# Opening of a decoder trunk's first FFN: order of scaling, high part, low part and modulation

## The chip, the cores and the metric

The kernel runs on one core of one Trainium2 chip. The metric is device time in microseconds (us) of one execution, from the profiler's clock. The time given for a kernel is the median of several executions; one further execution is profiled and gives the trace. Engine names: PE is TensorE (matmuls and transposes), ACT is ScalarE, DVE is VectorE, POOL is GpSimd, SP is the engine that issues the DMAs.

## The reference, cut to what matters

Two decoder layers on one sequence of 512 rows with 1024 channels; each layer is FFN, token mixer, FFN. Every sub-layer normalizes its input and modulates it by shift and scale that come from a conditioning vector. Only the start of the first FFN matters here:

```
cond = silu(c)
mod  = (cond @ ada_w[i] + ada_b[i]).reshape(b_, N_SUBLAYERS, 3, D_MODEL)
h = rms_norm(x, norm_g[i, 0]) * (1.0 + mod[:, 0, 1]) + mod[:, 0, 0]
g, u = jnp.split(h @ ffn_w_in[i, 0], 2, axis=-1)
x = x + 0.5 * (1.0 + mod[:, 0, 2]) * ((silu(g) * u) @ ffn_w_out[i, 0])
```

All is float32. The kernel keeps the precision by splitting each operand in a high part (rounded to the matmul's format) and a low part (what is left), and by three matmuls per product: high by high, low by high, high by low.

## The kernel before, in words

Channels lie on the 128 partitions, in KT = 8 groups kt of 128; the 512 rows lie along the free dimension, in four blocks b of 128. `hhi[:, kt]` and `hlo[:, kt]` are the high and low part of the modulated input of group kt. The FFN's hidden channels come in units j of 128, each with a gate half and an up half (k = 0, 1), so each unit needs two PSUM banks of 128x512 for its sums over kt.

There are eight PSUM banks. `bank("s")` takes one of three (pool `pss`), `bank("mm")` one of five (pool `ps`). A bank is free for the next tile when the last instruction that uses the one before it is done.

The opening (L724 to L793) runs as follows.

- L724 to L731: SP issues the loads of the rows (four blocks of 128x1024), of the identity, of the conditioning vector, of the first modulation weights and of the small vectors.
- L733 to L738: ACT squares the rows and sums them, DVE and POOL make the scale `v` of each row.
- L762 to L767: the row blocks are scaled by `v`, all 1024 channels at once, blocks 1 and 3 on ACT, 0 and 2 on DVE.
- `ada_work` (L97 to L103) and `ada_affine` (L113 to L122), both on DVE, make the modulation of one channel group from 1 MB of weights: two products with sums of 128x1024 and three tiny instructions. The last, L122, writes the shift `ms`.
- `by_channel(kt)` (L756): PE transposes the four 128x128 blocks of group kt into an `s` bank, and ACT copies the bank to SBUF (`x[:, kt]`, L760).
- `some_weights(kt, first, last)` (L744): for the units j from first to last, SP loads the weights of the groups kt and kt + 1 (256 KB), ACT makes their high part (L752), DVE their low part (L753).
- The loop over kt (L772 to L787): ACT makes `t1` from the copy with scale and shift (L774) and rounds it to `hhi` (L776); at kt = 0 the weights of units 2 and 3 and the copy of group 1 follow; then the transposes and copy of group kt + 2, the modulation of group kt + 1, and after it, on DVE, `hlo` (L785); at even kt then the weights of the next two groups, all four units.
- L788 to L793: eight banks for the sums of units 0 to 3, and 192 matmuls: for each kt 4 units x 2 halves x 3 matmuls (`mm3`, L163 to L165). The first three banks (unit 0 both halves, unit 1 the gate half) are `s` banks, the other five `mm` banks. The `s` pool hands out its banks in the order of the requests, so the three sums come after the eight transposed groups.

What sets the order: SP, DVE and ACT run their instructions in the order in which the program writes them (L718, `manual_schedule`); each engine waits at the first instruction that is not ready. PE's order is made when the kernel is built, by a planner that works with estimated times; on the chip PE runs that list in order.

After the opening, `ffn` (L258) goes on: the first four units are gated (`gated`, L286), then each further unit takes its weights from `Feed`, which loads them (L157) and splits them (L151 on ACT, L152 on DVE) into the slots that earlier units free, and `up` makes 48 matmuls per unit.

Of the kernel before, what the change touches and what calls it, by code (L numbers as in the profile page):

```python
# [7 lines left out]
F32 = mybir.dt.float32  # L8
F32R = mybir.dt.float32r
AF = mybir.ActivationFunctionType  # L10
ALU = mybir.AluOpType
# [4 lines left out]
P = 128  # L16
D = 1024
KT = D // P
S = 512
# [21 lines left out]
def trunk(  # L41
# [6 lines left out]
    pe, act, dve, gp = nc.tensor, nc.scalar, nc.vector, nc.gpsimd  # L48

    top = ctx.enter_context(tc.tile_pool(name="top", bufs=1, side="right"))  # L50
    hhi = top.tile([P, KT, S], F32R, name="hhi")
    hlo = top.tile([P, KT, S], F32R, name="hlo")
# [12 lines left out]
    def bank(tag="mm"):  # L65
        return banks[tag].tile([P, S], F32, tag=tag, name=tag)
# [11 lines left out]
    ident = pers.tile([P, P], F32, name="ident")  # L78
    ng = pers.tile([P, DEPTH * 3, KT], F32, name="ng")
    ab = pers.tile([P, DEPTH * 3, 3 * KT], F32, name="ab")  # L80
    x = pers.tile([P, KT, S], F32, name="x")
# [8 lines left out]
    mods = {}  # L90

    def ada_load(i, u, pool):
        raw = pool.tile([P, 2, D], F32, tag="ada", name="ada")
        nc.sync.dma_start(raw, ada_w[i, u])
        return raw
# [620 lines left out]
    with tc.tile_pool(name="more", bufs=1, side="right", reuse_waits="tile") as more:  # L716
        slots.update(pools=[wts, wts, more], at=1)
        in_order = tc.manual_schedule(  # L718
            engines={mybir.EngineType.SP, mybir.EngineType.DVE, mybir.EngineType.Activation})
        with tc.tile_pool(name="start", bufs=2, reuse_waits="tile") as sp, in_order, ExitStack() as early:  # L720
            adas0 = early.enter_context(tc.tile_pool(name="adas", bufs=5, reuse_waits="tile"))
            w4 = early.enter_context(tc.tile_pool(name="w4", bufs=1, reuse_waits="tile"))

            rows = sp.tile([P, NTB, D], F32, name="rows", bufs=1)  # L724
            for b in range(NTB):
                nc.sync.dma_start(rows[:, b], x_rows[:, b])
            nc.sync.dma_start(ident, consts[:, 0])
            nc.sync.dma_start(cond, c_in.to_broadcast([P, D]))
            first_ada = ada_load(0, 0, adas0)
            nc.sync.dma_start(ng, norm_g)  # L730
            nc.sync.dma_start(ab, ada_b)  # L731
            v = sp.tile([P, NTB], F32, name="v", bufs=1)
            for b in range(NTB):  # L733
                junk = x[:, 2 * b:2 * b + 2].rearrange("p a t -> p (a t)")
                act.activation(junk, rows[:, b], AF.Square, accum_out=v[:, b:b + 1])
            act.activation(cond, cond, AF.Silu)
            dve.tensor_scalar(out=v, in0=v, scalar1=1.0 / D, scalar2=EPS, op0=ALU.mult, op1=ALU.add)
            gp.tensor_tensor(out=v, in0=v, in1=mhalf[:, :NTB], op=ALU.pow)  # L738
            wt = [slot([P, 2, KT, P]) for _ in range(3)]
            wt.append(tuple(w4.tile([P, 2, KT, P], F32R, name="w" + t) for t in "hl"))  # L740

            pieces = {}

            def some_weights(kt, first=0, last=4):  # L744

                sl = slice(kt, kt + 2)
                if first == 0:
                    pieces[kt] = wts.tile([P, 4, 2, 2, P], F32, tag="raw", name="raw")
                for j in range(first, last):
                    (wh, wl), raw = wt[j], pieces[kt][:, j]  # L750
                    nc.sync.dma_start(raw, w_in[0, j, :, :, sl])
                    act.activation(wh[:, :, sl], raw, AF.Copy)  # L752
                    dve.tensor_tensor(out=wl[:, :, sl], in0=raw, in1=wh[:, :, sl].bitcast(F32),  # L753
                                      op=ALU.subtract)

            def by_channel(kt):  # L756
                t = bank("s")
                for b in range(NTB):
                    pe.transpose(t[:, b * P:(b + 1) * P], rows[:, b, kt * P:(kt + 1) * P], ident)
                act.activation(x[:, kt], t, AF.Copy)  # L760

            for b in range(NTB):  # L762
                if b % 2:
                    act.activation(rows[:, b], rows[:, b], AF.Copy, scale=v[:, b:b + 1])
                else:
                    dve.tensor_scalar(out=rows[:, b], in0=rows[:, b], scalar1=v[:, b:b + 1],
                                      scalar2=None, op0=ALU.mult)  # L767
            ada_work(0, 0, first_ada)
            ada_affine(0, 0, 1)
            by_channel(0)  # L770
            some_weights(0, 0, 2)
            for kt in range(KT):  # L772
                t1 = sp.tile([P, S], F32, tag="t1", name="t1")
                act.activation(t1, x[:, kt], AF.Identity, scale=mods[0]["a"][:, kt:kt + 1],  # L774
                               bias=mods[0]["s"][:, kt:kt + 1])
                act.activation(hhi[:, kt], t1, AF.Copy)  # L776
                if kt == 0:
                    some_weights(0, 2)
                    by_channel(1)
                if kt + 2 < KT:  # L780
                    by_channel(kt + 2)
                if kt + 1 < KT:
                    ada_work(0, kt + 1, ada_load(0, kt + 1, adas0))
                    ada_affine(0, kt + 1, 1)
                dve.tensor_tensor(out=hlo[:, kt], in0=t1, in1=hhi[:, kt].bitcast(F32), op=ALU.subtract)  # L785
                if kt % 2 == 0 and kt + 2 < KT:
                    some_weights(kt + 2)  # L787
            gu = [[bank("s" if 2 * j + k < 3 else "mm") for k in range(2)] for j in range(4)]  # L788
            for kt in range(KT):
                for j in range(4):  # L790
                    for k in range(2):
                        mm3(gu[j][k], wt[j][0][:, k, kt], wt[j][1][:, k, kt], hhi[:, kt], hlo[:, kt],
                            kt == 0, kt == KT - 1)  # L793

        def begin(g, gated):
            for j in range(4):
                gated(gu[j], g[j], 0, S)

        ahead = []

        def normed(i, w):
            def then(acc, t0, tn):
                if t0 and w is not None:
                    ahead.append(Feed(w))
                    ahead[0].fetch(len(slots["pools"]))
                norm(i, acc, t0, tn)

            return then

        with tc.tile_pool(name="poolw", bufs=1, side="right", reuse_waits="tile") as pw:  # L810
            pw_all = pw.tile([P, 16, P], F32, name="poolw")
            pooling = []
            opened = ExitStack()

            def pool_then(acc, t0, tn):
                r = rsig(acc, t0, tn)
                if t0 == 0:
                    pool = opened.enter_context(tc.tile_pool(name="pool", bufs=1, reuse_waits="tile"))
                    pooling.append(Pooling(1, pool, pw_all))
                    pooling.append(pooling[0].means(r, t0, tn))  # L820
                    return
                sums = pooling[0].mix(pooling[1], *HALVES[0])
                made = pooling[0].means(r, t0, tn)
                norm(2, sums, *HALVES[0], True)
                sums = pooling[0].mix(made, t0, tn)
                ahead.append(Feed(1))
                ahead[0].fetch(len(slots["pools"]))
                norm(2, sums, t0, tn, True)
                opened.close()

            jobs = ada_jobs(0, False) + ada_jobs(1)
            jobs += [(lambda pool: nc.sync.dma_start(pw_all, pool_w), lambda _: None)] + ada_jobs(2)
            feed = Feed(0)
            feed.units = feed.units[4:]
            ffn(0, feed, jobs, pool_then, begin, started=4)
        ffn(2, ahead.pop(), ada_jobs(3) + ada_jobs(4), normed(3, 2))
        fox_early = ctx.enter_context(tc.tile_pool(name="foxe", bufs=2, reuse_waits="tile"))
        first, first_jobs = fox_first(fox_early)
        held = []

        def fox_then(acc, t0, tn):
            if t0:
                held.append(lambda: norm(4, acc, t0, tn))
            else:
                norm(4, acc, t0, tn)

        ffn(3, ahead.pop(), ada_jobs(5) + first_jobs, fox_then, ahead_by=1)
# [68 lines left out]
```

## Time and profile before

| | |
|---|---|
| median of 3 executions | 1816.23 us (1815.08 to 1818.02) |
| profiled execution, its own time | 1816.93 us |
| its span, first to last instruction | 1815.2 us |
| PE busy | 1780.4 us, 98% of the span |
| DVE busy | 990.0 us, 55% |
| ACT busy | 622.1 us, 34% |

The profile lists for each instruction the start, the duration, the line, what it writes and reads, and how long its engine stood idle before it and which engine or DMA ended that. The span leaves out what lies before the first and after the last instruction, so it is 1.7 us below the execution's time. Shares of busy time are means over the whole span; a change in one stretch is read from the instructions of that stretch.

### The profile page before, as it was taken

Reading aid. Unit: us, or ns where it says so; the run is one execution under the profiler, and the core shown is the slowest. Engines: PE = TensorE matmul, PEld = TensorE weight load, DVE = VectorE, ACT = ScalarE, POOL = GpSimd, SP = SyncE. Lnnn points to the kernel's source line nnn. Section 1 sums busy time; section 2 is a strip of 40 time slices with the busy share of each in tenths; the row PEclk is TensorE's granted clock in tenths of the full one; section 3 lists DMA queues with packets and bytes.
Section 4 is the critical chain, followed back from the end, with each engine's and each line's share of the span. In section 5 each row is a group of like instructions: output and inputs, shape, how many; then the busy total and the mean of one; then the engine's idle time right before and its main releaser. Section 6 shows DMA issues by size and latency. Waiting matters only on the chain.

```text
span 1815.2 us, 24017 instructions
## 1 busy us (share of the span) xinstructions
PE 1780.4 (98%) x9564; PEld 1533.2 (84%) x9564; DVE 990.0 (55%) x1963; ACT 622.1 (34%) x1258; POOL 107.3 (6%) x118
## 2 busy tenths in 40 slices
PE   6999999989999999999999999999999999999999
PEld 4888888889888888998888889989998888888887
DVE  7567566376466563373544543667777653433333
ACT  6323223344223222242232232355554442222231
POOL 0000000050000000110000001311110200000000
PEclk9999999989999999999999999999999999999999
DMA  9457466220457453123353442112222121331421
GB/s 366 194 197 279 174 231 245 94 70 30 152 215 276 163 210 138 71 86 124 140 208 116 177 160 81 52 55 72 80 71 76 47 93 60 130 110 49 139 93 70
DMA packets 45857, 244.73 MB, mean 135 GB/s; under 512 B 5409, under 2 KB 10017, under 8 KB 21937
## 3 DMA queue, kind: packets, MB, share of 16 engines
q1 hardware_dynamic: 45744, 243.20, 36.6%
q8 instruction: 75, 1.23, 0.3%
q14 instruction: 38, 0.30, 0.1%
HBM read 241.05 MB, written 2.13 MB: 134 GB/s over the span
## 4 chain that ended last, share of the span: by engine, by line
PE 94%; DVE 4%; ACT 1%; DMA 1%; issue 0%; POOL 0%; SPq 0%; DVEq 0%; ACTq 0%; POOLq 0%
PE mm L164 27%; PE mm L165 27%; PE mm L163 27%; PE s L163 3%; PE s L164 3%; PE s L165 2%; PE mm L593 1%; DVE wl L152 1%; PE mm L619 1%; PE mm L596 1%; PE mm L422 1%; DVE x L225 0%; DMA rows<-x_rows 0%; DVE t L387 0%; DVE win L396 0%
## 5 line engine op out<-in xcount | busy, mean ns | idle before, releaser
L164 PE MATMUL mm<-hlo,wh 128*128 128x512 f32 (+1 forms) x1512 | 560.7, 372 | 2.8 <-DVE hlo L785 2.8
L165 PE MATMUL mm<-hhi,wl 128*128 128x512 f32 (+1 forms) x1512 | 558.3, 372 | 0.5 <-DVE wl L152 0.5
L163 PE MATMUL mm<-hhi,wh 128*128 128x512 f32 (+1 forms) x1512 | 554.4, 372 | 2.1 <-ACT hhi L776 1.8
L151 ACT ACTIVATE wh<-raw 128x256 fp32r<-128x256 f32 (+2 forms) x528 | 311.5, 654 | 567.4 <-PE mm L164 308.6
L152 DVE TENSOR_TENSOR wl<-raw,wh 128x256 fp32r<-128x256 f32 (+2 forms) x528 | 359.6, 735 | 52.3 <-ACT wh L151 48.1
L164 PEld LDWEIGHTS mm<-hlo,wh 128*128 128x128 f32 x1512 | 284.6, 188 | 52.3 <-DVE hlo L785 3.4
L163 PEld LDWEIGHTS mm<-hhi,wh 128*128 128x128 f32 x1512 | 282.8, 189 | 52.5 <-ACT hhi L776 2.0
L165 PEld LDWEIGHTS mm<-hhi,wl 128*128 128x128 f32 x1512 | 284.5, 188 | 49.9 <-DVE wl L152 0.7
L290 DVE TENSOR_TENSOR sil<-sil,mm 128x512 f32<-128x512 f32 (+1 forms) x95 | 61.0, 642 | 463.1 <-PE mm L165 454.5
L164 PE MATMUL mm<-gl,wh 128*128 128x512 f32 (+1 forms) x848 | 299.1, 353 | 0.0
L165 PE MATMUL mm<-gh,wl 128*128 128x512 f32 (+1 forms) x848 | 298.4, 353 | 0.0
L163 PE MATMUL mm<-gh,wh 128*128 128x512 f32 (+1 forms) x848 | 297.9, 354 | 0.0
L164 PEld LDWEIGHTS mm<-gl,wh 128*128 128x128 f32 x848 | 160.4, 189 | 21.9
L165 PEld LDWEIGHTS mm<-gh,wl 128*128 128x128 f32 x848 | 160.4, 189 | 21.8
L163 PEld LDWEIGHTS mm<-gh,wh 128*128 128x128 f32 x848 | 159.7, 189 | 22.0
L100 DVE CUSTOM_DVE_ANT_0 ada<-ada,cond 128x1024 f32<-128x1024 f32 x144 | 170.2, 1220 | 0.5 <-DMA ada<-ada_w 0.5
L289 ACT ACTIVATE sil<-mm 128x512 f32<-128x512 f32 (+1 forms) x94 | 52.7, 560 | 245.1 <-PE mm L165 243.9
L337 DVE SCALAR_TENSOR_TENSOR x<-mm,mg,x 128x512 f32<-128x512 f32 x64 | 48.0, 750 | 103.2 <-PE mm L165 102.2
L175 POOL TENSOR_TENSOR acc<-acc,sq 128x256 f32<-128x256 f32 x56 | 49.8, 889 | 845.0 <-ACT sq L174 513.9
L163 PE MATMUL s<-wh,hhi 128*128 128x256 f32 x288 | 84.6, 294 | 0.0
L165 PE MATMUL s<-wh,hlo 128*128 128x256 f32 x288 | 82.0, 285 | 0.0
L164 PE MATMUL s<-wl,hhi 128*128 128x256 f32 x288 | 81.9, 285 | 0.0
(173 smaller groups left out, 1633.7 us busy)
## 6 DMA issues: line engine op xcount, KB each, us to landing
raw<-w_in SPq DMA_DIRECT2D x84, 1024.0 KB, 4.9
ada<-ada_w SPq DMA_DIRECT2D x72, 1024.0 KB, 4.9
raw<-w_out SPq DMA_DIRECT2D x64, 512.0 KB, 5.6
raw<-w_end SPq DMA_DIRECT2D x12, 1024.0 KB, 4.9
raw<-fox_qkv SPq DMA_DIRECT2D x12, 1024.0 KB, 4.8
raw<-w_in SPq DMA_DIRECT2D x16, 256.0 KB, 8.0
cb<-cum SPq DMA_DIRECT2D x16, 256.0 KB, 3.4
raw<-fox_o SPq DMA_DIRECT2D x4, 1024.0 KB, 4.9
```

The source lines that it names most:

```text
L100: dve.tensor_tensor_reduce(out=raw[:, r, :], in0=raw[:, r, :], in1=cond, scale=1.0, scalar=0.0, op0=ALU.mult, op1=ALU.add, accum_out=mods[ ...
L151: act.activation(hi[:, c:c + n], src[:, c:c + n], AF.Copy)
L152: dve.tensor_tensor(out=lo[:, c:c + n], in0=src[:, c:c + n], in1=hi[:, c:c + n].bitcast(F32), op=ALU.subtract)
L163: pe.matmul(o, lh, rh, start=start, stop=False)
L164: pe.matmul(o, lh, rl, start=False, stop=False)
L165: pe.matmul(o, ll, rh, start=False, stop=stop)
L175: gp.tensor_tensor(out=acc[:, sl], in0=acc[:, sl], in1=sq, op=ALU.add)
L289: act.activation(sil[:, :tn], gu[0][:, :tn], AF.Silu)
L290: dve.tensor_tensor(out=sil[:, :tn], in0=sil[:, :tn], in1=gu[1][:, :tn], op=ALU.mult)
L337: done = dve.scalar_tensor_tensor(out=x[:, dt, :], in0=y, scalar=mods[i]["g"][:, dt:dt + 1], in1=x[:, dt, :], op0=ALU.mult, op1=ALU.add)
L422: pe.matmul(y[:, :tn], self.w[:, 2 * dt + ct], made[dt // 2][:, ct], start=ct == 0, stop=ct == 1)
L593: pe.matmul(s[hh][:, :n], self.q[m == 2][rows, self.pair, b * P:n], self.k[m == 1][rows, self.pair, :n], start=m == 0, stop=False)
```

## The change

Seven edits, all in the opening. Rows are scaled in two steps: first the channels 0 to 255 of all four blocks, then, later and all on ACT, the other 768 (blocks 1 and 3 ahead of the first modulation, blocks 0 and 2 at the end of kt = 0). The copy of each transposed bank to SBUF goes. `hhi` is made by one ACT instruction straight from the PSUM bank (`high`), and `t1` by a second one from the same bank (`whole`). The first `high` stands between the weights of unit 0 and unit 1. `hlo` moves ahead of the next group's modulation. The weights of the later groups are split two units at a time: units 0 and 1 of groups kt + 1 and kt + 2 at odd kt, units 2 and 3 at the even kt that follows, in both cases ahead of `hlo`.

```diff
-            def some_weights(kt, first=0, last=4):
+            def some_weights(kt, first, last, between=None):
...
                     act.activation(wh[:, :, sl], raw, AF.Copy)
                     dve.tensor_tensor(out=wl[:, :, sl], in0=raw, in1=wh[:, :, sl].bitcast(F32),
                                       op=ALU.subtract)
+                    if between and j == first:
+                        between()
 
             def by_channel(kt):
-                t = bank("s")
+                turned[kt] = bank("s")
                 for b in range(NTB):
-                    pe.transpose(t[:, b * P:(b + 1) * P], rows[:, b, kt * P:(kt + 1) * P], ident)
-                act.activation(x[:, kt], t, AF.Copy)
-
+                    pe.transpose(turned[kt][:, b * P:(b + 1) * P], rows[:, b, kt * P:(kt + 1) * P], ident)
+
+            def scaled(b, c0, c1, on_act):
+                part = rows[:, b, c0:c1]
+                if on_act:
+                    act.activation(part, part, AF.Copy, scale=v[:, b:b + 1])
+                else:
+                    dve.tensor_scalar(out=part, in0=part, scalar1=v[:, b:b + 1], scalar2=None, op0=ALU.mult)
+
+            def high(kt):
+                act.activation(hhi[:, kt], turned[kt], AF.Identity, scale=mods[0]["a"][:, kt:kt + 1],
+                               bias=mods[0]["s"][:, kt:kt + 1])
+
+            def whole(kt):
+                t1 = sp.tile([P, S], F32, tag="t1", name="t1")
+                act.activation(t1, turned.pop(kt), AF.Identity, scale=mods[0]["a"][:, kt:kt + 1],
+                               bias=mods[0]["s"][:, kt:kt + 1])
+                return t1
+
+            turned = {}
+            soon = 2 * P
             for b in range(NTB):
-                if b % 2:
-                    act.activation(rows[:, b], rows[:, b], AF.Copy, scale=v[:, b:b + 1])
-                else:
-                    dve.tensor_scalar(out=rows[:, b], in0=rows[:, b], scalar1=v[:, b:b + 1],
-                                      scalar2=None, op0=ALU.mult)
+                scaled(b, 0, soon, b % 2)
+            by_channel(0)
+            for b in (1, 3):
+                scaled(b, soon, D, True)
             ada_work(0, 0, first_ada)
             ada_affine(0, 0, 1)
-            by_channel(0)
-            some_weights(0, 0, 2)
+            some_weights(0, 0, 2, lambda: high(0))
+            by_channel(1)
             for kt in range(KT):
-                t1 = sp.tile([P, S], F32, tag="t1", name="t1")
-                act.activation(t1, x[:, kt], AF.Identity, scale=mods[0]["a"][:, kt:kt + 1],
-                               bias=mods[0]["s"][:, kt:kt + 1])
-                act.activation(hhi[:, kt], t1, AF.Copy)
+                if kt:
+                    high(kt)
+                t1 = whole(kt)
+                if kt % 2 and kt + 1 < KT:
+                    some_weights(kt + 1, 0, 2)
+                elif kt % 2 == 0 and kt:
+                    some_weights(kt, 2, 4)
+                dve.tensor_tensor(out=hlo[:, kt], in0=t1, in1=hhi[:, kt].bitcast(F32), op=ALU.subtract)
                 if kt == 0:
-                    some_weights(0, 2)
-                    by_channel(1)
+                    some_weights(0, 2, 4)
+                    for b in (0, 2):
+                        scaled(b, soon, D, True)
                 if kt + 2 < KT:
                     by_channel(kt + 2)
                 if kt + 1 < KT:
                     ada_work(0, kt + 1, ada_load(0, kt + 1, adas0))
                     ada_affine(0, kt + 1, 1)
-                dve.tensor_tensor(out=hlo[:, kt], in0=t1, in1=hhi[:, kt].bitcast(F32), op=ALU.subtract)
-                if kt % 2 == 0 and kt + 2 < KT:
-                    some_weights(kt + 2)
```

## Rows read from the trace of the kernel before

**Rows 1.** The page's first line: span.

```profile
span 1815.2 us, 24017 instructions
```

**Rows 2.** Stretches from:to: length, PE, PEld, DVE, ACT, POOL busy, clock, DMA share, GB/s.

```profile
0.00:28.64 28.64, 11.62 (x49) 8.67 (x49) 16.02 (x36) 19.20 (x30) 1.31 (x6) 0.94 0.98 356
28.64:68.66 40.02, 40.02 (x177) 32.62 (x177) 25.54 (x54) 18.58 (x31) 0.00 (x0) 1.00 0.47 183
```

**Rows 3.** Timeline of PE: start, duration, instruction, [idle before, what ended it].

```profile
17.70 2.26 PE L163 MATMUL mm<-hhi,wh 128*128 128x512 f32 x5 [1.78 <-ACT hhi L776]
19.76 1.91 PE L759 MATMUL s<-ident,rows 128*128 128x128 f32 x8
22.89 0.50 PE L164 MATMUL mm<-hlo,wh 128*128 128x512 f32 x1 [1.22 <-DVE hlo L785]
...
28.64 0.50 PE L164 MATMUL mm<-hlo,wh 128*128 128x512 f32 x1 [1.57 <-DVE hlo L785]
...
36.13 0.39 PE L163 MATMUL s<-hhi,wh 128*128 128x512 f32 x1
...
68.66 0.48 PE L163 MATMUL mm<-hhi,wh 128*128 128x512 f32 x1
```

**Rows 4.** Timeline of DVE in the opening, same columns.

```profile
13.24 1.23 DVE L100 CUSTOM_DVE_ANT_0 ada<-ada,cond 128x1024 f32<-128x1024 f32 x1 [0.46 <-DMA ada<-ada_w]
...
15.93 0.15 DVE L122 COPY ms<-mraw 128x1 f32<-128x1 f32 x1
...
19.41 1.22 DVE L100 CUSTOM_DVE_ANT_0 ada<-ada,cond 128x1024 f32<-128x1024 f32 x1
...
22.15 0.68 DVE L785 TENSOR_TENSOR hlo<-t,hhi 128x512 fp32r<-128x512 f32 x1
22.75 2.49 DVE L753 TENSOR_TENSOR wl<-raw,wh 128x512 fp32r<-128x512 f32 x4
25.16 1.22 DVE L100 CUSTOM_DVE_ANT_0 ada<-ada,cond 128x1024 f32<-128x1024 f32 x1
...
27.84 0.15 DVE L122 COPY ms<-mraw 128x1 f32<-128x1 f32 x1
27.90 0.68 DVE L785 TENSOR_TENSOR hlo<-t,hhi 128x512 fp32r<-128x512 f32 x1
28.50 1.22 DVE L100 CUSTOM_DVE_ANT_0 ada<-ada,cond 128x1024 f32<-128x1024 f32 x1
```

**Rows 5.** Timeline of ACT in the opening, same columns.

```profile
15.10 1.14 ACT L752 ACTIVATE wh<-raw 128x512 fp32r<-128x512 f32 x2
...
28.02 0.81 ACT L774 ACTIVATE t<-x,ms,ma 128x512 f32<-128x512 f32 x1 [3.66 <-DVE ms L122]
28.87 0.63 ACT L776 ACTIVATE hhi<-t 128x512 fp32r<-128x512 f32 x1
29.41 0.58 ACT L760 ACTIVATE x<-s 128x512 f32<-128x512 f32 x1
...
37.11 0.82 ACT L774 ACTIVATE t<-x,ms,ma 128x512 f32<-128x512 f32 x1 [3.18 <-DVE ms L122]
```

**Rows 6.** Groups by line and form, ACT: count | busy us, mean ns | idle before.

```profile
L752 ACT ACTIVATE wh<-raw 128x512 fp32r<-128x512 f32 x16 | 9.2, 623 | 0.3
L774 ACT ACTIVATE t<-x,ms,ma 128x512 f32<-128x512 f32 x8 | 6.5, 812 | 11.9 <-DVE ms L122 11.9
L776 ACT ACTIVATE hhi<-t 128x512 fp32r<-128x512 f32 x8 | 5.1, 632 | 0.3
L760 ACT ACTIVATE x<-s 128x512 f32<-128x512 f32 x8 | 4.6, 583 | 0.8 <-PE s L759 0.8
L764 ACT ACTIVATE rows<-rows,v 128x1024 f32<-128x1024 f32 x2 | 2.2, 1134 | 0.0
```

**Rows 7.** Stretches as in rows 2, around the first matmuls: granted clock.

```profile
20.00:22.00 2.00, 1.67 (x8) 1.27 (x6) 1.94 (x5) 1.68 (x4) 0.00 (x0) 0.50 1.12 421
22.80:28.64 5.84, 4.18 (x20) 3.24 (x20) 5.77 (x14) 2.15 (x4) 0.00 (x0) 1.00 1.05 391
```

## The prediction

> **What bounds the kernel now.** I read the stretches first. After 28.64 us PE is never idle until the sums of the first four units are done at 68.66, where the first matmul of the fifth unit starts: 40.02 us busy in 40.02 [rows 2]. Before 28.64 it works 11.62 of 28.64 us. So PE's work sets the end of the opening, and only idle time of PE ahead of 28.64 can be won. The timeline of PE shows it: 1.78 us ahead of the first matmul (released by `hhi`), 1.22 at 22.89 and 1.57 at 28.64 (both released by `hlo`) [rows 3]. On DVE the order behind the last two is plain: the modulation of the next group, begun at 19.41 and at 25.16, is done ahead of `hlo` at 22.15 and at 27.90 [rows 4]. The same order has a good side. While ACT makes `t1` and `hhi`, DVE works on the next modulation and never waits for ACT; ACT waits for DVE instead, 11.9 us in all at `t1` [rows 6]. Two groups take DVE from ACT's `t1` at 28.02 to the one at 37.11, so 4.55 us a group [rows 5]. PE's price of a matmul in this stretch: 172 of the 192 matmuls are still to do at 28.64 (five at 17.70 and 15 from 22.89 on have run) and four transposes of some 0.15 us, so (40.02 - 0.6) / 172 = 0.229 us, 5.5 us for the 24 of a group [rows 2, 3]. DVE's 4.55 a group keeps ahead of that.
>
> **The change part by part.**
>
> *First scaling.* DVE's first modulation starts at 13.24, when its DMA lands, not when DVE is free [rows 4]. Two scalings made shorter on DVE ahead of it gain nothing. On ACT the split rows cost two extra instructions; a whole one takes 1.134 us for 1024 columns, a half-width weight instruction 0.623 for 512, so the fixed part is some 0.11 to 0.2 each [rows 6]. ACT is through with them some 1.7 us before the first `ms` is there (15.93 + 0.15 = 16.08 [rows 4]). The high part of unit 0's weights fits between: its data were there by 15.10 at the latest [rows 5], and 0.62 later is 15.72. Cost nothing, covered by the wait for `ms`; without that cover, under 0.5 us.
>
> *High part from PSUM.* No row has an Identity with scale and bias out of PSUM. Below, a plain copy out of PSUM, 0.583; above, the Identity out of SBUF, 0.812 [rows 6]. I take 0.583 plus what scale and bias add in SBUF (0.812 - 0.632 = 0.18), 0.76. ACT instructions that don't depend on one another overlap by 0.09 (0.63 after 28.87 is 29.50, the next starts at 29.41 [rows 5]), so `high` and `whole` take 0.67 each in sequence, 0.49 to 0.72 by the bounds. `hhi` of group 0 is ready at 16.1 + 0.8 = 16.9 where the first matmul now starts at 17.70: PE starts 0.8 us earlier. The eight copies that go (0.583 each) lay on an engine with 11.9 us of waits; nothing is won.
>
> *Group 0's low part.* ACT: `high` to 16.9, weights of unit 1 to 17.4, `whole` to 18.1. DVE: `hlo` at 18.1 to 18.8 instead of 22.15 to 22.83. The stall of 1.22 us goes. Then the two weight pieces of units 2 and 3 (0.60 each: four take 25.16 - 22.75 = 2.41 [rows 4]) and the modulation of group 1, from 19.95 instead of 19.41. It takes 27.99 - 25.16 = 2.83 to the end of `ms` [rows 4]: 22.78, half a microsecond later than now. The late scaling of blocks 0 and 2 on ACT (two of some 0.9) ends near 21, hidden in ACT's wait for that `ms`.
>
> *The order inside the loop.* Here I see the price. From group 1 on, the program order is, on ACT: `high`, `whole`, two weight pieces; on DVE: the two low pieces, `hlo`, the next modulation. ACT's `high` waits for `ms`; DVE's low pieces wait for ACT's pieces, which stand behind `high` and `whole`. Behind DVE's first waiting piece are queued `hlo` and the whole next modulation. So the two engines take turns, and the loop is one chain: 0.03 to ACT, 0.67 `high`, 0.67 `whole`, 0.62 first weight piece, 0.03 to DVE (ACT's 28.02 is 0.03 behind the end of `ms` at 27.99 [rows 4, 5]), 1.20 two low pieces, 0.60 `hlo` (28.50 - 27.90 [rows 4]), 2.83 modulation. Sum 6.65 us a group against 4.55 now; 6.3 to 6.75 by the bounds of `high` and `whole`. `ms` of group 5 is then at 22.78 + 4 x 6.65 = 49.4, of group 7 at 62.7.
>
> *The banks.* Now each `s` bank is free after the copy of its group, which ACT makes two groups ahead; the first matmul into an `s` bank is at 36.13 [rows 3]. After the change a bank is held until `whole` of its group. The three sums in `s` banks take the banks of groups 5, 6 and 7. So until `whole` of group 5, at 51, PE has only five of the eight sums to work on: 15 matmuls, 3.4 us, and four transposes per 6.65 us. It is idle for a third of the time, with everything else waiting for the chain.
>
> *PE's end.* When `hhi` of group 5 is there, at 49.4 + 0.8 = 50.2, five sums x 5 groups x 3 = 75 matmuls are done and 117 are left. From here PE has work all the time (10 matmuls of group 5 until the first `s` bank is free at 51, then 18 more in that bank, then group 6): 117 x 0.229 = 26.8 us, end at 77.0 where it is 68.66 now. Sum: 8.3 us later. What follows (gating, the split of the next weights into freed slots) hangs on the same last matmuls in the same order, and shifts with them.
>
> *DMA queue.* Weight loads go two at a time between the modulation loads, the same bytes. DVE takes everything later than now from group 2 on, so landings have more room; a load behind a buffer wait (groups 6 and 7's weights wait for those of 2 and 3, freed near 33) still has some 18 us to its use. Nothing. POOL has no part in the loop.
>
> Total: 1816.93 (the profiled execution; span 1815.2 [rows 1], the rest lies around it) + 8.3 = 1825.2. The median is 0.7 below that execution, so **1824.5**. By the bounds of `high` and `whole` the end moves by 4.5 times theirs per group, about -1.6 to +0.5: 1823 to 1825.
>
> **The clock, row against rule.** The first five matmuls ran at the low level, start to start (19.76 - 17.70) / 5 = 0.41 us, and the granted clock was 0.50 (1.2 GHz) from 20 to 22 and 1.00 (2.4 GHz) from 22.8 on, across a gap of 1.57 us [rows 3, 7]. In my forecast PE has gaps of up to 2.4 us per group, and no row here shows such gaps repeated; I take the high level. The Trainium skill, "TensorE: Matmul & The Clock Gate", section on HAM oscillation, describes the opposite for matmul bursts with a wait per K-tile: each wait can send the clock back to half, and each burst starts cold. By that rule the time would be rival C's, not 1824.5.
>
> **Rivals.**
>
> *A, faster.* The edits do what the stalls ask for: 0.8 us earlier start, 1.22 and 1.57 gone, 3.6 us in all, **1812.9**. It holds if the loop's chain is short enough. Point of decision: PE ends at 68.66 if `hhi` of group 5 comes by 68.66 - 26.8 = 41.9, so `ms` by 41.1, so a loop of (41.1 - 22.78) / 4 = 4.6 us. That is DVE's own work per group (1.20 + 0.60 + 2.74): ACT's 2 us would have to vanish wholly from the chain, as now. For it: only that ACT has time to spare. Against: in-order engines. Chance 0.08.
>
> *B, no change.* The loop lengthens, but the `s` banks come free early (the pool finds others, or the order of requests is not what the code says). Then all eight sums follow each group, PE needs 5.5 of 6.65 us, and the end hangs on the last group: `hhi` at 63.5 + 24 x 0.229 = 69.0, **1816.6**. Against: three banks and the first `s` matmul now coming only after the last transposes but two. Chance 0.10.
>
> *C, slower still.* The same chain, with PE at 1.2 GHz during the bursts. 15 matmuls at 0.41 and transposes (0.24 each, 1.91 for eight [rows 3]) take 7.1 per 6.65 us, so some backlog, up to 1.5 us; and from 50 on the low level lasts up to 5 us, as from 17.70 to 22.8 [rows 3, 7], which costs half of it. Plus 2 to 4: **1826.5 to 1828.5**. The build-time order of PE, if it puts a matmul ahead that isn't ready, adds the same way. Chance 0.17.
>
> **How the numbers follow.** My forecast has 0.62 (1823 to 1825.5); the rest, 0.03, is a smaller delay of 3 to 6 us. The range from 1819 to 1829 takes in C and the smaller delay and leaves out A and B. About 0.2% (3.6 us) is what a measurement of this kernel can tell from no change. Faster by more: A, 0.08. Within: B and a part of the smaller delay, 0.11. Slower: 0.81.
>
> **What would show it.** Right: DVE idle by some 2 us in each group at the low weight pieces, released by ACT's high pieces; `ms` every 6.65 us; PE idle between 22 and 50 for the chain; the first `s` matmul near 51; no PE gap after that, fifth unit near 77. Wrong: `ms` every 4.6 us, or `s` matmuls before 45, or 1.2 GHz rows between 25 and 55.

## The result and the profile after

The changed kernel takes 1829.18 us (median of 4, 1828.89 to 1831.73) against 1816.24; the ratio is 1.0072, 95% interval 1.006 to 1.0084. That is 12.9 us slower. The forecast was 8.3 us, with a range up to 1829.0: the sign and the main mechanism came out, the size did not. About a third of the loss lies where the prediction had put nothing.

The profiled executions, 1827.6 us of span against 1815.2 [rows 1], tell where the 12.4 us between them arise. I count the opening from the end of the first `ms`, since that end hangs on when the first loads land: over the traces of this document it lies between 15.82 and 17.63 us.

| | before | after | difference |
|---|---|---|---|
| end of first `ms` | 16.08 | 15.93 | -0.15 |
| from there to the first matmul of the fifth unit | 52.58 | 62.80 | +10.22 |
| from there to the first norm instruction of the pooling mixer | 310.03 | 310.07 | +0.04 |
| from there to the table load in the attention layer | 807.00 | 810.23 | +3.23 |
| from there to the end | 629.51 | 628.57 | -0.94 |

The timeline of DVE in the changed kernel (start, duration, instruction, [idle before, what ended it]):

```profile
22.50 0.15 DVE L122 COPY ms<-mraw 128x1 f32<-128x1 f32 x1
24.74 1.29 DVE L753 TENSOR_TENSOR wl<-raw,wh 128x512 fp32r<-128x512 f32 x2 [2.09 <-ACT wh L752]
25.95 0.69 DVE L799 TENSOR_TENSOR hlo<-t,hhi 128x512 fp32r<-128x512 f32 x1
26.56 1.22 DVE L100 CUSTOM_DVE_ANT_0 ada<-ada,cond 128x1024 f32<-128x1024 f32 x1
...
29.23 0.15 DVE L122 COPY ms<-mraw 128x1 f32<-128x1 f32 x1
...
78.00 0.68 DVE L290 TENSOR_TENSOR sil<-sil,mm 128x512 f32<-128x512 f32 x1
```

From one `ms` to the next are 6.73 us, where the kernel before has 4.55 on average [rows 5]. In each round DVE now stands idle for 2.1 us, until ACT has made the first high weight piece. The timeline of ACT has the other half of the turn, and the end of the opening:

```profile
22.75 0.78 ACT L771 ACTIVATE hhi<-s,ms,ma 128x512 fp32r<-128x512 f32 x1 [2.07 <-DVE ms L122]
23.43 0.77 ACT L776 ACTIVATE t<-s,ms,ma 128x512 f32<-128x512 f32 x1
24.09 1.14 ACT L752 ACTIVATE wh<-raw 128x512 fp32r<-128x512 f32 x2
29.48 0.78 ACT L771 ACTIVATE hhi<-s,ms,ma 128x512 fp32r<-128x512 f32 x1 [4.25 <-DVE ms L122]
...
74.14 0.60 ACT L289 ACTIVATE sil<-s 128x512 f32<-128x512 f32 x1 [9.55 <-PE s L165]
74.64 2.00 ACT L151 ACTIVATE wh<-raw 128x1024 fp32r<-128x1024 f32 x2
76.53 0.59 ACT L289 ACTIVATE sil<-s 128x512 f32<-128x512 f32 x1
```

ACT waits 4.25 us for `ms`, then DVE waits 2.1 for ACT: of the 6.73 us of a round the two work together for only some 0.4. PE pays, in the changed kernel's timeline of PE:

```profile
17.36 0.79 PE L163 MATMUL mm<-hhi,wh 128*128 128x512 f32 x1 [3.79 <-ACT wh L752]
...
20.00 0.63 PE L165 MATMUL mm<-hhi,wl 128*128 128x512 f32 x1
20.42 1.05 PE L164 MATMUL mm<-hlo,wh 128*128 128x512 f32 x2
...
27.15 0.39 PE L165 MATMUL mm<-hhi,wl 128*128 128x512 f32 x1
27.38 0.40 PE L164 MATMUL mm<-hlo,wh 128*128 128x512 f32 x1
...
37.04 1.42 PE L163 MATMUL mm<-hhi,wh 128*128 128x512 f32 x5 [1.01 <-ACT hhi L771]
...
40.16 0.50 PE L164 MATMUL mm<-hlo,wh 128*128 128x512 f32 x1 [1.26 <-DVE hlo L799]
...
51.76 0.40 PE L163 MATMUL s<-hhi,wh 128*128 128x512 f32 x1
...
77.14 0.39 PE L165 MATMUL mm<-hhi,wl 128*128 128x512 f32 x1
78.73 0.50 PE L163 MATMUL mm<-hhi,wh 128*128 128x512 f32 x1 [1.21 <-DVE sil L290]
```

From 30 to 51 PE waits twice per group, for `hhi` and for `hlo`; the first matmul into an `s` bank comes at 51.76 instead of 36.13, the last of the 192 matmuls starts at 77.14; and then there is a new wait of 1.21 us ahead of the fifth unit, which starts at 78.73 instead of 68.66 [rows 3]. The stalls of 1.22 and 1.57 us in [rows 3] are gone, as the change meant them to be, and others stand in their place.

### The profile page after: what moved, and what is told of

It is laid out like the page before. It is cut to its first block, busy times and chain, and to the rows that moved or that the text cites. A ratio compares the mean times of both kernels' runs of the same rounds, so it can differ in the third digit from the quotient of the medians.

```text
span 1827.6 us, 24025 instructions
## 1 busy us (share of the span) xinstructions
PE 1784.7 (98%) x9564; PEld 1533.7 (84%) x9564; DVE 990.8 (54%) x1963; ACT 620.3 (34%) x1254; POOL 107.3 (6%) x118
## 4 chain that ended last, share of the span: by engine, by line
PE 93%; DVE 4%; ACT 1%; issue 1%; DMA 1%; SPq 0%; POOL 0%; ACTq 0%; DVEq 0%; POOLq 0%
PE mm L163 27%; PE mm L164 27%; PE mm L165 27%; PE s L163 3%; PE s L164 2%; PE s L165 2%; PE mm L593 1%; DVE wl L152 1%; PE mm L619 1%; PE mm L422 1%; DVE ada L100 1%; PE mm L596 1%; DMA ada<-ada_w 1%; DVE win L396 0%; DVE x L225 0%
## 5 line engine op out<-in xcount | busy, mean ns | idle before, releaser
L289 ACT ACTIVATE sil<-mm 128x512 f32<-128x512 f32 (+1 forms) x94 | 52.8, 561 | 244.5 <-PE mm L165 241.7
L291 ACT ACTIVATE gh<-sil 128x512 fp32r<-128x512 f32 (+1 forms) x96 | 55.9, 584 | 77.4 <-DVE sil L290 77.3
```

What stands on the lines that cost most here:

```text
L289: act.activation(sil[:, :tn], gu[0][:, :tn], AF.Silu)
L291: act.activation(g[0][:, sl], sil[:, :tn], AF.Copy)
```

## The experiments

All the runs below were made beside runs of the kernel before on the same chip. The table gives what each kernel's trace and times show; the first two lines are the kernels above. "Fifth unit" is counted from the end of the first `ms`, "stage" is the stretch from the first norm instruction of the pooling mixer to the table load.

| run | `ms` every, us | first `s` matmul | fifth unit | stage, us | median, us | ratio to before, interval |
|---|---|---|---|---|---|---|
| before | 4.55 | 36.13 | 52.58 | 807.00 | 1816.24 | |
| after | 6.73 | 51.76 | 62.80 | 810.23 | 1829.18 | 1.0072, 1.006 to 1.0084 |
| e1 old order | 4.55 | 46.04 | 55.18 | 807.20 | 1818.43 | 1.0011, 1.0002 to 1.002 |
| e2 copy back | 6.81 | 42.42 | 61.23 | 806.46 | 1825.01 | 1.0045, 1.003 to 1.006 |
| e3 weights first | 5.01 | 45.12 | 54.53 | 806.28 | 1817.24 | 1.0004, 0.9994 to 1.0014 |
| e4 weights first, copy | 5.09 | 40.98 | 55.90 | 809.50 | 1823.37 | 1.0034, 1.0021 to 1.0047 |
| e5 late banks | 6.73 | 52.44 | 61.65 | 807.30 | 1825.84 | 1.0056, 1.0041 to 1.0071 |
| e6 late banks, weights first | 5.01 | 45.30 | 54.69 | 805.82 | 1818.28 | 1.0015, 1.0006 to 1.0024 |
| p1 before, pinned | 4.54 | 36.01 | 52.59 | 869.81 | 1878.34 | 1.0349, 1.0332 to 1.0366 |
| p2 after, pinned | 6.73 | 52.76 | 62.82 | 869.82 | 1888.54 | 1.0402, 1.0387 to 1.0418 |
| e7 copy from 5 | 5.01 | 40.41 | 52.87 | 812.19 | 1820.80 | 1.0021, 1.0012 to 1.003 |
| e8 copy from 5, late banks | 5.01 | 39.92 | 53.05 | 806.52 | 1816.10 | 0.9999, 0.999 to 1.0008 |

### The loop and the banks

**e1, the loop's old order.** In the loop of the changed kernel:

```diff
                 t1 = whole(kt)
-                if kt % 2 and kt + 1 < KT:
-                    some_weights(kt + 1, 0, 2)
-                elif kt % 2 == 0 and kt:
-                    some_weights(kt, 2, 4)
-                dve.tensor_tensor(out=hlo[:, kt], in0=t1, in1=hhi[:, kt].bitcast(F32), op=ALU.subtract)
...
                     ada_affine(0, kt + 1, 1)
+                dve.tensor_tensor(out=hlo[:, kt], in0=t1, in1=hhi[:, kt].bitcast(F32), op=ALU.subtract)
+                if kt % 2 == 0 and kt + 2 < KT:
+                    some_weights(kt + 2, 0, 4)
```

> The changed kernel with the loop's old order on DVE and ACT: hlo behind the next modulation again, the weights of two groups four units at a time behind it. Direct high part from PSUM, banks held until the second read, and scaling in two steps stay. Theory 1 (the loss is the turn-taking of ACT and DVE together with the held banks): ms comes every 4.5 to 4.6 us again instead of 6.73, and with it the held banks come free soon enough; the fifth unit starts at 68 to 70.5 us instead of 78.73. Theory 2 (the held banks alone starve PE, whatever the loop): the first matmul into an s bank stays after 50 and the fifth unit starts at 75 or later.

The timeline of PE in this run:

```profile
46.04 0.39 PE L163 MATMUL s<-hhi,wh 128*128 128x512 f32 x1
...
71.59 0.47 PE L163 MATMUL mm<-hhi,wh 128*128 128x512 f32 x1
```

`ms` comes every 4.55 us again on average, and 7.6 of the 10.2 us are back (62.80 to 55.18). Theory 2, that the banks alone starve PE, falls. Theory 1 is right in kind, but its number is missed by 1.1 us (71.59, expected up to 70.5; 0.5 of that is a later first `ms`): 2.6 us stay. The first `s` matmul is 10 us later than before, so the banks held for the second read are the suspect; e3 and e7 below differ in just three of these banks, and by 1.7 us.

**e2, the copy put back**, so that each bank is free when its group is copied:

```diff
                     pe.transpose(turned[kt][:, b * P:(b + 1) * P], rows[:, b, kt * P:(kt + 1) * P], ident)
+                act.activation(x[:, kt], turned[kt], AF.Copy)
+                turned[kt] = x[:, kt]
```

> The changed kernel with the copy of each transposed bank to SBUF put back, so that high and whole read the copy and the bank is free two groups earlier; the new order of the loop stays. Theory 1: ms still every 6.6 to 6.8 us, but all eight sums can follow each group; the first matmul into an s bank comes near 43 instead of 51.8, and the fifth unit starts at 69.5 to 72 instead of 78.73. Theory 3 (the slow loop alone sets the end, the banks don't matter): fifth unit within 1 us of 78.7.

Only 1.6 us come back, and neither theory has the fifth unit right (77.05 on the clock). The first `s` matmul is as early as expected (42.42, expected near 43). But only 50 of the 192 matmuls are done by then, and the other 142, with the transposes, keep PE busy for the 33.2 us to the wait ahead of the fifth unit (77.05 less 1.41); I had only counted the last group. And the copies brought a wait of their own, in this run's timelines of ACT and PE:

```profile
25.24 0.60 ACT L762 ACTIVATE x<-s 128x512 f32<-128x512 f32 x1 [4.10 <-PE s L761]
```

```profile
23.70 0.81 PE L761 MATMUL s<-ident,rows 128*128 128x128 f32 x6
```

The copy of group 2 waits for its transposes, and `high` of group 1 stands behind it on ACT. The late scaling of the rows is over at 21.14; the transposes come from 23.70 on because in PE's order they stand behind matmuls of group 0, which start some 0.43 us apart until 22.6. That delays the `ms` of group 2 once, to 9.32 us behind that of group 1, and puts each later `ms` 3.2 to 3.6 us behind its place in the changed kernel, counted from the first. So this run mixes free banks with a later loop: the 1.6 us do not tell what free banks alone are worth. Theory 3 is the nearer one, off by 1.7 us, but it is not shown.

**e3, weights first.** The two calls of `some_weights` are put ahead of `high`; ACT then makes the pieces while it waits for `ms`, and DVE makes the low pieces while ACT makes `high` and `whole`. `hlo` stays ahead of the next modulation.

```diff
+                if kt % 2 == 0 and kt:
+                    some_weights(kt, 2, 4)
+                elif kt % 2 and kt + 1 < KT:
+                    some_weights(kt + 1, 0, 2)
                 if kt:
                     high(kt)
                 t1 = whole(kt)
-                if kt % 2 and kt + 1 < KT:
-                    some_weights(kt + 1, 0, 2)
-                elif kt % 2 == 0 and kt:
-                    some_weights(kt, 2, 4)
```

> The changed kernel with the two weight pieces of each group moved ahead of high in the program, so that ACT makes them while it waits for ms and DVE makes the low pieces while ACT makes high and whole; hlo stays ahead of the next modulation, banks stay held. Theory 1: the loop is then modulation 2.83, high and whole 1.4, hlo 0.6, so ms every 4.8 to 5.1 us; hhi of group 5 near 43.5; fifth unit at 70 to 72.5. Theory 2 (held banks alone): 75 or later.

`ms` every 5.01 us, the fifth unit at 70.69: both as theory 1 has it. Two of the rows, from its timeline of DVE:

```profile
27.75 0.15 DVE L122 COPY ms<-mraw 128x1 f32<-128x1 f32 x1
...
32.76 0.15 DVE L122 COPY ms<-mraw 128x1 f32<-128x1 f32 x1
```

This is the closest test of the mechanism: nothing but the place of two weight pieces in the source differs from the changed kernel, and 8.3 of the 10.2 us are gone. The pace of the loop is a matter of ACT and DVE, which run in the written order. The end of the opening is also PE's, and PE's order, made at build, moved with the edit: in the traces 84 of its 224 instructions up to the fifth unit stand at another place. What is left shows in its timeline of PE and in the stretch from 30 to 45 us (length, busy us of PE, PEld, DVE, ACT, POOL, clock, DMA share, GB/s):

```profile
33.84 1.43 PE L163 MATMUL mm<-hhi,wh 128*128 128x512 f32 x5 [0.82 <-ACT hhi L771]
...
45.12 0.40 PE L163 MATMUL s<-hhi,wh 128*128 128x512 f32 x1
```

```profile
30.00:45.00 15.00, 12.54 (x59) 9.36 (x58) 13.66 (x31) 7.43 (x13) 0.00 (x0) 1.00 0.96 375
```

PE is idle 2.46 of these 15 us. That it is for want of `s` banks is tested by e7 below.

**e4, both.**

> Weights ahead of high as in the run before, and the copy of each bank put back. Theory 1: ms every 4.8 to 5.1 us, banks free two groups earlier; PE starts at 17.0 to 17.4, has small stalls, fifth unit at 67 to 69.5, about where the kernel before has it (68.66). The whole time then differs from the kernel before by that and by what the planner makes of the pooling stage (3.3 us more in the changed kernel than in the one before).

The loop's pace is as expected, the fifth unit is not: 55.90 us behind the first `ms`, 1.4 more than without the copies (73.53 on the clock, expected 67 to 69.5; the first `ms` is 1.7 us later than in the changed kernel). As in e2 the copy of group 2 holds ACT up, by 4.2 us, once. Here the copies cost more than the banks that they free are worth.

**e7 and e8, the copy for the groups 5 to 7 alone.** These are the groups whose banks the first sums take, and by then the transposes are in time.

```diff
+                if kt >= 5:
+                    act.activation(x[:, kt], turned[kt], AF.Copy)
+                    turned[kt] = x[:, kt]
```

> Weights ahead of high, direct reads from PSUM for the groups 0 to 4, and the copy of the bank put back for the groups 5, 6 and 7 alone, whose banks the first three sums take. Theory 1 (with the loop at 5.0 us, what is left of the loss is PE's idle time between 30 and 45 us for want of s banks, 2.5 us): ms every 5.0 us, first s matmul at 35 to 38 instead of 45.1, PE busy over 14.3 of the 15 us from 30 to 45; counted from the first ms, the fifth unit 51 to 52.8 us later (kernel before 52.6, weights first alone 54.5). Rival: the copies hold ACT up as in the two runs with all copies, the loop falls to 5.3 us or more and nothing is won.

> The same with the s banks given to the last three sums. Theory 1: as the run before, first matmul 0.5 us sooner after the first ms; the fifth unit 50.5 to 52.5 us after the first ms. Against the kernel before -2 to 0 us from the opening, plus what the planner makes of the pooling stage (so far between -1.2 and +3.3 us).

The same stretch in e7 and in e8, one row each:

```profile
30.00:45.00 15.00, 14.17 (x67) 11.08 (x67) 13.64 (x31) 8.46 (x15) 0.00 (x0) 1.00 0.98 380
```

```profile
30.00:45.00 15.00, 13.86 (x66) 10.88 (x65) 13.64 (x31) 8.46 (x15) 0.00 (x0) 1.00 0.97 378
```

PE gets back 1.6 us of the 2.46 in e7 and 1.3 in e8, a little less than expected (14.3 busy), and the first `s` matmul is at 40, not 35 to 38. The rival falls, since from group 1 on `ms` comes at most 5.09 us apart. The fifth unit misses its range by 0.1 us in e7 (52.87, expected up to 52.8) and by 0.6 in e8 (53.05, up to 52.5); the opening is where the kernel before has it (52.58), so neither is faster there. The two differ by 0.2 us in the opening and by 4.7 us in the whole. That difference has its own section below.

### The wait ahead of the fifth unit

The fifth unit needs an `mm` bank. In the changed kernel unit 0's two sums are in `s` banks, so the first `mm` bank comes free only with the gating of unit 1. The rows above show its way: ACT's `sil` of unit 1 at 76.53, behind the high part of the next weights, DVE's product at 78.00 to 78.68, PE at 78.73. The kernel before has the same order, and there it fits by a hair (its timelines of ACT and DVE; the fifth unit starts at 68.66):

```profile
64.05 0.60 ACT L289 ACTIVATE sil<-s 128x512 f32<-128x512 f32 x1 [13.02 <-PE s L165]
```

```profile
67.91 0.68 DVE L290 TENSOR_TENSOR sil<-sil,mm 128x512 f32<-128x512 f32 x1
```

From unit 0's `sil` to the fifth unit are 4.61 us before and 4.59 after. But before, PE still had matmuls of the other units for all of that time; in the changed kernel they are over 3.4 us behind that `sil` (78.73 less 1.21 is 77.52).

**e5** gives the three `s` banks to the last three sums:

```diff
-            gu = [[bank("s" if 2 * j + k < 3 else "mm") for k in range(2)] for j in range(4)]
+            gu = [[bank("s" if 2 * j + k > 4 else "mm") for k in range(2)] for j in range(4)]
```

> The changed kernel with the three s banks given to the last three of the eight sums (unit 3 and the up half of unit 2) instead of the first three. The loop stays, ms every 6.73 us. Theory 1 (the fifth unit waits for the gating of the first units, whose sums end late since unit 0 sits in the late banks; and the first matmul waits for unit 1's weights since unit 0 has no early bank): first matmul at 16.7 to 17.0 instead of 17.36, no idle time of PE ahead of the fifth unit, which starts at 76.5 to 77.7 instead of 78.73. Theory 5 (that wait is set by PE's end, not by the order of the sums): first matmul and gap as in the changed kernel, fifth unit within 0.4 us of 78.7.

```profile
17.51 2.50 PE L163 MATMUL mm<-hhi,wh 128*128 128x512 f32 x5 [3.29 <-ACT hhi L771]
...
78.23 0.39 PE L163 MATMUL mm<-hhi,wh 128*128 128x512 f32 x1
```

In this timeline of PE the fifth unit starts with no idle time ahead of it, 61.65 us behind the first `ms` instead of 62.80. On the clock it is 78.23, outside the expected 77.7, since the first `ms` came 0.65 us later (16.58). The first matmul follows the first `ms` by 0.93 us instead of 1.43: it waits for `hhi`, no longer for unit 1's weights. One half of my reason was wrong: unit 0's sums end no sooner (its `sil` is 58.4 us behind the first `ms` in this run, 58.2 in the changed kernel). What counts is that its gating now frees `mm` banks.

**e6** joins this with the weights first.

> Both together: weights ahead of high, late sums in the s banks, direct reads from PSUM kept. ms every 5.0 us as in the run with weights first. Theory 1: first matmul near 16.9, fifth unit at 68.5 to 70.2 (70.69 with weights first alone); against the kernel before -0.5 to +1.5 us from the opening, plus what the planner makes of the pooling stage.

The first matmul is 0.92 us behind `ms`, but the fifth unit at 54.69 gains nothing over e3 (54.53): without the wait at the end, and with PE short of banks from 30 to 45, there is nothing for the swap to win. 71.03 on the clock misses the expected 70.2.

### The stage that nobody touched

The pooling mixer takes 3.23 us more after the change, though no line of it differs. The planner lays out PE, DVE, ACT and POOL there by estimated times. The traces show that its order is another one: in this stage, some 150 of PE's 4200 instructions stand in other places than before, and some 65 of DVE's 783. To see whether this order is the cause, p1 and p2 keep the written order for this stage, in the kernel before and in the changed one; there, the traces of the two have the same instructions in the same order on all four engines.

```diff
-                    closing(feed.made, 6, g, i, acc, then)
+                    with (tc.manual_schedule(engines={
+                            mybir.EngineType.DVE, mybir.EngineType.Activation,
+                            mybir.EngineType.PE, mybir.EngineType.Pool})
+                          if i == 0 else ExitStack()):
+                        closing(feed.made, 6, g, i, acc, then)
```

> The kernel before, with the last stage of the first FFN and the pooling mixer behind it in the written order on DVE, ACT, POOL and PE instead of the planner's. Theory 1 (the changed opening also made the planner lay out this stage in another way, which costs 3.2 us in the changed kernel): the stage may become longer or shorter than 807 us from its first norm instruction to the table load in the attention layer, but by the same amount as in the next run; opening as in the kernel before, fifth unit within 0.3 us of 68.7.

> The changed kernel with the same stage in the written order. Theory 1: the stage takes as long as in the run before within 0.5 us, and the two kernels differ by the opening alone, about 10.1 us (9.3 to 10.8). Theory 4 (the later loss is no matter of the planner but follows from the late opening, through DMA or clock): they still differ by 12 to 13.5 us.

First and last instruction of the stage, by the timelines of DVE and ACT, in the kernel before, the changed one, p1 and p2:

```profile
378.69 0.87 DVE L387 SCALAR_TENSOR_TENSOR t<-x,ma,s 128x256 f32<-128x256 f32 x2
...
1185.69 1.28 ACT L485 ACT_TABLE_LOAD   x1
```

```profile
388.80 0.87 DVE L387 SCALAR_TENSOR_TENSOR t<-x,ma,s 128x256 f32<-128x256 f32 x2
...
1199.03 1.28 ACT L485 ACT_TABLE_LOAD   x1
```

```profile
377.98 0.87 DVE L391 SCALAR_TENSOR_TENSOR t<-x,ma,s 128x256 f32<-128x256 f32 x2 [1.23 <-PE s L207]
...
1247.79 1.28 ACT L489 ACT_TABLE_LOAD   x1
```

```profile
389.22 0.87 DVE L391 SCALAR_TENSOR_TENSOR t<-x,ma,s 128x256 f32<-128x256 f32 x2 [1.23 <-PE s L207]
...
1259.04 1.28 ACT L489 ACT_TABLE_LOAD   x1
```

The written order is a bad one, 63 us longer. But it is the same for both: 869.81 and 869.82 us, and the two medians differ by 10.2 us, the opening's price. With the planner's order they differ by 12.9; the intervals of these times are too wide to tell 10.2 from 12.9, so it is the length of the stage that tells. Theory 4 falls: a late opening alone does not lengthen this stage.

The planned kernels bear this out, and show a limit. By the traces, three pairs of them run the stage in the very same order on all four engines: the changed kernel and e7 (810.23 and 812.19 us), e1 and e3 (807.20 and 806.28), e5 and e6 (807.30 and 805.82). The order of the changed kernel has the two longest stages of the ten planned kernels, once behind a late opening and once, in e7, behind an early one; e5 has a late opening and a short stage. In the changed kernel's order PE waits longer for the pooled parts, as the waits of PE show for 376 to 440 us before and 386 to 450 after (us in total, times, longest):

```profile
PE mm L422 <- DVE made L412: 0.3, 1, 0.3
```

```profile
PE mm L422 <- DVE made L412: 2.7, 2, 1.9
```

The first 70 us of the stage, before and after, with the columns of the stretches above:

```profile
378.69:448.69 70.00, 62.52 (x397) 56.67 (x397) 58.29 (x124) 32.15 (x72) 20.91 (x19) 0.93 0.13 46
```

```profile
388.80:458.80 70.00, 60.56 (x370) 54.41 (x370) 56.72 (x121) 29.14 (x67) 20.83 (x19) 0.90 0.13 46
```

So 2.0 of the 3.2 us are idle time of PE. The rest is not all a matter of order, since the same order still gives stages 0.9 to 2.0 us apart. In e1 and e3, for example, PE stands idle for the same 4.57 us near the start of the pooling; the 8 us that begin 14.5 us behind the first norm instruction are, in e1 and in e3:

```profile
396.14:404.14 8.00, 7.42 (x20) 5.98 (x19) 7.95 (x17) 0.83 (x2) 1.86 (x3) 0.50 0.37 132
```

```profile
395.26:403.26 8.00, 7.19 (x28) 5.73 (x27) 7.96 (x18) 0.92 (x3) 1.86 (x3) 0.83 0.37 133
```

With a granted clock of 0.50 (1.2 GHz) PE comes through 20 matmuls of the same list, with 0.83 (in part at 2.4 GHz) through 28. So the order is shown to matter here, but not how much of the 3.2 us it makes by itself, and the 0.01 us between p1 and p2, from one trace each, are closer than such pairs are. The medians point the same way: with the opening's part taken off, the changed kernel is 2.7 us above the kernel before and e7 4.3, e4 3.6, and the other six planned kernels lie between -1.1 and +0.9. Over all ten the stage is between 805.8 and 812.2 us long; e7 and e8 are the plainest pair, with 812.19 and 806.52.

## Why the prediction was wrong

- *The chain.* Right. The forecast was 6.65 us per group, DVE idle 2 us at the low weight pieces, `hhi` of group 5 at 50.2, the first `s` matmul near 51; measured 6.73, 2.1, 50.46 and 51.76. `high` and `whole` take 0.78 and 0.77 us and follow each other by 0.68 and 0.67, where I had taken 0.67. That this order is the cause is shown by e1 and e3, which give back 7.6 and 8.3 of 10.2 us by the written order alone. These include the wait of 1.4 us ahead of the fifth unit (see the first step that failed), which is gone in both, and what PE's own order, moved with them, made of it.
- *PE's end.* The 117 matmuls from `hhi` of group 5 on, forecast to end at 77.0, ended at about 77.4 (77.14 and one distance of 0.23). That term, 8.3 us in the sum, measured 8.7.
- *First step that failed:* "What follows ... hangs on the same last matmuls in the same order, and shifts with them." It doesn't hang on the last matmuls, but on the `mm` bank that the gating of unit 1 frees. Before, that fell together with PE's end. In the changed kernel it comes 1.4 us later than PE's end (68.66 to 78.73 is 10.07, against 8.7). e5 removes the wait.
- *Second step that failed:* the sum ends with the opening. It names the order made at build only as a part of rival C, within PE's stretch of the opening, and gives the rest of the program nothing. The pooling stage took 3.2 us more. p1 and p2, and e7 with the same order behind an early opening, show that the planner's order there lengthens it, and not the later time; 2.0 of the 3.2 us are idle time of PE, and part of the rest can be the granted clock of the one execution. The cause of the 0.94 us that come back behind the table load stays open; pinned, that stretch is 628.5 us in both kernels, and over all twelve traces it is between 627.4 and 629.6.
- *PE's start.* Forecast 16.9, measured 17.36. The idea was that `hhi` goes ahead of unit 1's weights. But the first sum in an `mm` bank is unit 1's, so PE waits for just these weights. e5 and e8 start 0.5 us sooner. It was worth nothing in the end: PE starves behind it.
- *The rivals.* A fell with the loop's 6.73 us, B with the first `s` matmul at 51.76. (A's time is off by a slip: 3.6 us below 1816.23 is 1812.6, not 1812.9.) For C, the distance of the matmuls tells: 0.43 us apart at 20, 0.23 at 27, and 0.23 from there on. So 1.2 GHz at the start and 2.4 GHz from 25 on, all through PE's idle spells of 0.7 to 1.3 us, two per group. C's time of 1826.5 to 1828.5 was nearest to the result, for the wrong reason. The rule of the Trainium skill ("TensorE: Matmul & The Clock Gate", section on HAM oscillation), that bursts with a wait per K-tile can fall back to the slow clock each time, did not come into play: the DMA waits of that section's example are longer than the gaps here, and no group of the changed kernel fell back in the opening after 25 us.

## What to carry to other kernels

Where two engines run in program order, look at each place where one waits for the other and ask what work that does not depend on the wait stands behind it: here two weight pieces that needed nothing from the modulation made a pipeline take turns, and moving them ahead of the wait gave back 8.3 of the 10.2 us that the opening had lost. When a buffer's holder is changed, follow which consumer gets which buffer up to the next stage, not just to the end of the loop. And where a planner orders the program from estimates, a change in one stage can reorder another; compare the orders, or pin one for both kernels, before a difference of a few us is read as the change's own. Compare also two runs of the same order, to see how far they lie apart without any cause in the program.

## What the runs showed of the hardware

The granted clock of the profile does not always follow the matmuls. In the changed kernel's stretch from 18 to 22 us it reads 1.00, while matmuls of 512 columns start 0.43 us apart (20.00 and 20.42 above), near the 0.41 that the prediction reads off at a granted clock of 0.50 (1.2 GHz); at 27 us they start 0.23 apart with the same reading:

```profile
18.00:22.00 4.00, 3.61 (x9) 2.77 (x9) 4.00 (x7) 2.67 (x4) 0.00 (x0) 1.00 1.04 400
```

In the kernel before, the same reading was 0.50 from 20 to 22 [rows 7]. Here the distance of the starts is the safer sign. Reading the operand from PSUM instead of SBUF made ACT's Identity with scale and bias some 0.03 us shorter (0.78 against 0.812 [rows 6], and 0.80 to 0.82 in e2).
